# A third landing slot for weights, paid for with a staging slot, in a two-layer hybrid backbone

## The chip, the cores and the metric

The kernel runs on one core of one Trainium2 chip, as one launch. The metric is the device time of that launch in microseconds (us), less is better. The engines are named as in the profile: PE (TensorE, matrix products), PEld (its weight loads), DVE (VectorE), ACT (ScalarE), POOL (GpSimd) and SP (SyncE, which here only issues DMAs; SPq and ACTq are the queues of the two engines that issue them).

## The reference, cut to what matters

Two layers, each over 1024 latent tokens and 256 context tokens of width 1024, all in float32:

```python
for l in range(DEPTH):                                   # DEPTH = 2
    shift, scale, gate = split(silu(c) @ w_ada[l] + b_ada[l], 3)
    h = layer_norm(x) * (1 + scale) + shift              # the context rows likewise
    q, k, v, g_att, u_conv, g_conv, x_lru, g_lru = split_in_proj(h @ w_in[l])
    ys = window_attention(q, k, v, ...), conformer_conv(u_conv, ...), rglru(x_lru, ...)
    y = stack([yb * silu(gb) for yb, gb in zip(ys, gs)])   # three branches, 512 wide each
    proj = einsum('btnw,nwd->btnd', y, w_branch[l])
    g = sigmoid(h @ w_gate[l] + b_gate[l])                 # one gate per branch and channel
    out = sum(proj * g, branches) @ w_out[l]
    x = layer_norm(ALPHA * x + gate * out) * ln_g[l] + ln_b[l]
```

The big products are h with w_in (3840 columns) and w_gate (3072 columns), the branches with w_branch, and the merge with w_out.

## The kernel before

**Weights.** Every big product is made in three matmuls of a cheaper format: a float32 operand is split into a high part and the rest. A weight unit (class `Wt`, 128 x 1024 elements, 512 KB) goes through four steps in `Wt.load`: a DMA on SP into a tile `raw` (L332 is that DMA's line in the profile), a copy on ACT that rounds it to `whi`, a subtraction on DVE that leaves the rest in `wlo`, and then matmuls with both. Each of the three has a ring of slots in the pool W: `NWL` = 2 slots for raw, `NW` = 4 each for whi and wlo. A raw slot is free once the subtraction has read it; a whi and wlo slot is free once PE has used the unit. There are 180 such units. Four of each layer (half of w_out) live in another pool, RC, that is opened late in phase 2, and had `NW` = 4 raw slots there.

**Phase 1** of a layer (`phase1`) runs nine streams: gates, attention projection, scores, values and output, convolution, recurrence in, recurrence, recurrence out. `Driver.run` picks among them by its own cost estimates and emits their instructions in one long order. The products with w_gate and w_in interleave with all the rest. In layer 0 the gates' stream also computes the conditioning of layer 1 (`ada_pair`): two weight units of w_ada for each pair of column groups, used up in 32 short matmuls.

**Phase 2** (`phase2`) merges. The three branch outputs, which phase 1 left in DRAM (`yd`), come back in pieces of 128 x 512 through a ring of `NYST` = 3 staging slots (`yst`, L1156 is the DMA): `yfetch` fills the ring, `ysplit` splits one piece into high part and rest (ACT, then DVE; the tile is `yy`) and fetches the next. The order of branches is recurrence (i = 0), convolution (i = 1), attention (i = 2). The sigmoid values come back as `thl`. The sums of a row block stand in `m`: in tiles `mx` for latent tokens, and in a ring `mc` of four 2 KB slots for the context. Then come the two halves of the product with w_out, the second layer norm, and the transposed and modulated input of the next layer (`norm`: tiles `xp`, `hf`, `hlhi`). The tiles `tt` of the w_out product and `hf` share one ring of two slots in RC.

**Gate rows.** `gate_out` transposes the conditioning's gate into a row tile `grow`, copies it from PSUM on DVE and stores it to DRAM; `gate_in` later reads it back, spread over partitions. It is called at the start of the second and third quarter of branch i = 0. **First rows.** `load_c` brings the two conditioning vectors in at the very start, in tiles `crow` and `crow2`. All these row tiles are 512 bytes for each partition in a pool SM that stays open all the time.

**Order and waits.** Nothing in the code waits by hand. Tiles of one tag share that tag's slots, and an instruction that would write into a slot waits for the last reader of what stood there. The program is compiled with

```python
with _tile.TileContext(nc, schedule_with_timeline_sim=True) as tc:
```

so the order on each engine is not the order of emission: a list scheduler places each instruction when its operands and its slot are there in a simulated run, the earlier emitted first. What results is one fixed order for each engine and queue, and on the chip each of them works strictly through it: the profile shows an instruction that waits and everything behind it on its engine standing still. The pools s, h, a, b and c of the phases follow one another in the same memory, and a tile of a later pool waits for the tiles that lay there before.

Of the kernel before, what the change touches and what calls it, by code (L numbers as in the profile page):

```python
# [8 lines left out]
F32 = mybir.dt.float32  # L9
# [23 lines left out]
NT_1 = (2, C + 512, 512)  # L33

SLOT = 1408
NS, NHF, NW, NWL, NMX, NYST = 10, 14, 4, 2, 8, 3
LH = 6


# [150 lines left out]
def kernel(  # L190
# [14 lines left out]
    SM = ctx.enter_context(tc.tile_pool(name="small", bufs=1))  # L205
# [3 lines left out]
    def pad(pool_, n, tag):  # L209

        if n:
            pool.memset(pool_.tile([128, n // 4], F32, tag=tag, name=tag), 0.0)
# [6 lines left out]
    def f32(ap):  # L219
        return ap.bitcast(F32)  # L220

    def psum(n=512, name="ps"):
        return PM.tile([128, n], F32, tag="mm", name=name, bufs=4)
# [97 lines left out]
    class Wt:  # L321
# [6 lines left out]
            self.ap, self.ready = drv_.side(lambda: self.load(src, a, b, home or W))  # L328

        def load(self, src, a, b, home):  # L330
            raw = home.tile([128, a, b], F32, tag="raw", name="raw", bufs=NWL if self.own else NW)
            sp.dma_start(out=raw, in_=src)  # L332
            hi = home.tile([128, a, b], F32R, tag="whi", name="whi", bufs=NW)
            lo = home.tile([128, a, b], F32R, tag="wlo", name="wlo", bufs=NW)
            act.activation(out=hi, in_=raw, func=AF.Copy)
            dve.tensor_tensor(out=lo, in0=raw, in1=f32(hi), op=ALU.subtract)
            return hi, lo
# [14 lines left out]
    def split(src, hi, lo):  # L352
        act.activation(out=hi, in_=src, func=AF.Copy)
        dve.tensor_tensor(out=lo, in0=src, in1=f32(hi), op=ALU.subtract)
# [3 lines left out]
    sel = K.tile([4, 2], F32, tag="sel", name="sel")  # L358
    dve.tensor_tensor(out=sel, in0=ident[0:4, 0:2], in1=ident[0:4, 2:4], op=ALU.add)

    def load_c():
        rows = SM.tile([128, 128], F32, tag="crow", name="crow")
        sp.dma_start(out=rows[0:8], in_=c[0].rearrange("(r p) -> r p", p=128))
        sp.dma_start(out=rows[8:16], in_=c_ctx.rearrange("(r p) -> r p", p=128))
        t = SM.tile([128, 128], F32, tag="crow2", name="crow2")
        act.activation(out=t[0:16], in_=rows[0:16], func=AF.Tanh, scale=0.5)
        dve.scalar_tensor_tensor(out=t[0:16], in0=t[0:16], scalar=1.0, in1=rows[0:16], op0=ALU.add, op1=ALU.mult)
        dve.tensor_scalar(out=t[0:16], in0=t[0:16], scalar1=0.5, scalar2=None, op0=ALU.mult)
        ps = psum()
        pe.transpose(ps[:, 0:16], t[0:16], ident[0:16, 0:16])  # L370
        dve.tensor_copy(cs.rearrange("p k s -> p s k"), ps[:, 0:16].rearrange("p (s k) -> p s k", s=2))
        split(cs, csr[:, :, 0:2], csr[:, :, 2:4])
# [3 lines left out]
    def ada_fin(l, jjs, ps, rows, r):  # L376

        n = len(jjs) * 128
        act.activation(out=r[0:rows, 0:n], in_=ps[0:rows, 0:n], func=AF.Copy)
        for i in range(len(jjs)):  # L380
            pe.matmul(out=ps[:, 2 * i:2 * i + 2], lhsT=r[0:rows, i * 128:i * 128 + 128], rhs=sel[0:rows], start=True,
                      stop=True)
        part, m = jjs[0] // 8, len(jjs)
        dst = ada[l][:, jjs[0]:jjs[0] + m, :]
        bias = prm[l][:, P_ADA + jjs[0]:P_ADA + jjs[0] + m].unsqueeze(2).to_broadcast([128, m, 2])
        dve.scalar_tensor_tensor(out=dst, in0=ps[:, 0:2 * m].rearrange("p (m s) -> p m s", s=2),
                                 scalar=1.0 if part == 1 else 0.0, in1=bias, op0=ALU.add, op1=ALU.add)
        if part == 2:
            dve.tensor_scalar(out=dst, in0=dst, scalar1=0.25, scalar2=None, op0=ALU.mult)
# [35 lines left out]
    def alloc_h(ti, n):  # L425
        tg, b = ("hc", 2) if n == 256 else ("hl", 4)
        return tuple(H.tile([128, KD, n], F32R, tag=tg, name=f"{tg}{v}", bufs=b) for v in ("hi", "lo"))

    def emit_h0(R, P):
        tiles = [(ctxt, 0), (ctxt, 128)] + [(x, 128 * i) for i in range(8)]  # L430
        raws, xt = {}, {}
        nts = (NT_C, NT_0, NT_1)

        def load_x(i):
            t = R.tile([128, 2, 512], F32, tag="raw0", name="x0", bufs=17).rearrange("p a b -> p (a b)")
            sp.dma_start(out=t, in_=tiles[i][0][0, tiles[i][1]:tiles[i][1] + 128, :])
            xt[i] = t

        def load_ada(g, q):
            raws[g, q] = R.tile([128, 2, 512], F32, tag="raw0", name="raw0", bufs=17)  # L440
            sp.dma_start(out=raws[g, q], in_=w_ada[0][q * 256:q * 256 + 256, g * 512:g * 512 + 512].rearrange(
                "(k p) n -> p k n", p=128))

        rows_ = {}

        def ada_rows(g, q):
            if q == 0:
                rows_[g] = P.tile([128, 512], F32, tag="p0", name="pa", bufs=4)
            for k in range(2):
                pe.matmul(out=rows_[g][0:2], lhsT=cs[:, q * 2 + k, :], rhs=raws[g, q][:, k, :],  # L450
                          start=(q == 0 and k == 0), stop=(q == 3 and k == 1))
            if q == 3:
                ada_fin(0, [g * 4 + i for i in range(4)], rows_[g], 2,
                        R.tile([128, 512], F32, tag="hf0", name="arow", bufs=5))

        def norm_x(i):
            t = xt[i]
            mv, rs = ln_stats(t)
            nb = SM.tile([128, 1], F32, tag="nb", name="nb", bufs=3)
            dve.scalar_tensor_tensor(out=nb, in0=mv[:, 0:1], scalar=-1.0, in1=rs, op0=ALU.mult, op1=ALU.mult)  # L460
            act.activation(out=t, in_=t, func=AF.Identity, scale=rs, bias=nb)

        def modulate(j, nt):
            ti, t0, n = nt
            s = 1 if ti == 0 else 0
            ps = P.tile([128, 512], F32, tag="p0", name="p0", bufs=4)
            for i in range(n // 128):
                pe.transpose(ps[:, i * 128:i * 128 + 128], xt[t0 // 128 + i][:, j * 128:j * 128 + 128], ident)
            hf = R.tile([128, 512], F32, tag="hf0", name="hf0", bufs=5)
            act.activation(out=hf[:, 0:n], in_=ps[:, 0:n], func=AF.Identity, scale=ada[0][:, 8 + j, s:s + 1],  # L470
                           bias=ada[0][:, j, s:s + 1])
            hi, lo = (v[:, j, :] for v in hT[0, ti])
            if j < (4, 4, 6)[ti]:
                act.activation(out=hi, in_=hf[:, 0:n], func=AF.Copy)
            else:
                dve.tensor_copy(hi, hf[:, 0:n])
            dve.tensor_tensor(out=lo, in0=hf[:, 0:n], in1=f32(hi), op=ALU.subtract)

        load_c()
        for nt in nts:  # L480
            hT[0, nt[0]] = alloc_h(nt[0], nt[2])
            if nt is NT_C:
                pad(H, 64, "padh2")

        def rows_tile():
            return R.tile([128, 128], F32, tag="rows", name="rows", bufs=2)

        order = [("a", 0, 0), ("a", 0, 1), ("a", 0, 2), ("r",), ("a", 2, 0), ("a", 0, 3), ("a", 2, 1), ("a", 2, 2),
                 ("a", 2, 3), ("x", 0), ("x", 1), ("a", 1, 0), ("a", 1, 1), ("a", 1, 2), ("a", 1, 3), ("a", 3, 0),
                 ("a", 3, 1), ("a", 3, 2), ("a", 3, 3), ("m", NT_C, 0), ("m", NT_C, 4), ("x", 2), ("x", 3),  # L490
                 ("x", 4), ("x", 5), ("x", 8), ("m", NT_0, 0), ("m", NT_0, 4), ("x", 6), ("x", 9), ("x", 7),
                 ("m", NT_1, 0), ("m", NT_1, 4)]
        for what, *v in order:
            if what == "m":
                for j in range(v[1], v[1] + 4):
                    modulate(j, v[0])
            elif what == "r":
                load_params(0, *load_rows(0, rows_tile))
            elif what == "a":
                load_ada(*v)  # L500
                ada_rows(*v)
            else:
                load_x(*v)
                norm_x(*v)
# [622 lines left out]
        drv_.run([lru(), att_values(), att_scores(), lru_in(), lru_out(), att_proj(), att_out(), conv(), gates()], PRIO[l])  # L1127
        assert wlive[0] == 0 and sl.used == 0 and hl_.used == 0 and pl_.used == 0

    def gate_out(l, s):  # L1130

        row = SM.tile([128, 128], F32, tag="grow", name="grow")
        ps = psum()
        pe.transpose(ps[0:KD, 0:128], ada[l][:, 16:24, s], ident)
        dve.tensor_copy(row[0:KD], ps[0:KD, 0:128])
        sp.dma_start(out=gate_d[l][s].rearrange("(k p) -> k p", p=128), in_=row[0:KD])
# [5 lines left out]
    def phase2(l, open_a, open_b, open_c):  # L1142
# [24 lines left out]
        def mc(name):  # L1167
            return RB.tile([128, 512], F32, tag="mc", name=name, bufs=4)
# [52 lines left out]
        def gemm():  # L1221
# [3 lines left out]
            for i, b in enumerate(BR):  # L1225
                for dp in range(4):
                    if i == 0 and 0 < dp < len(groups):
                        gate_out(l, dp - 1)
                    if i == 0:
                        for nt in groups:  # L1230
                            if nt is NT_C:
# [232 lines left out]
```

## Time and profile before

| | |
|---|---|
| median of 3 runs | 2307.63 us (2306.44 to 2307.89) |
| time of the profiled execution | 2307.8 us |
| its span, first to last instruction | 2306.0 us |
| PE busy | 2249.3 us (98%) |
| DVE busy | 1678.9 us (73%) |
| ACT busy | 1003.4 us (44%) |
| mean granted TensorE clock | 0.990 |

The span is what the trace covers; 1.8 us of the profiled execution's time lie outside it. All times in the trace count from the first instruction. Almost every instruction has the line L73, which is the helper `Meter` that records costs; so the rows are read by the tiles, out<-in. Phase 1 of layer 0 begins at about 55 us, phase 2 is under way alone from 1021 us, layer 1 begins at about 1303 us, and its phase 2 at about 2078 us. Matmuls overlap in the pipeline, so PE's busy time counts small delays as work; idle times of PE are real.

### The profile page before, as it was taken

The page shows a single profiled execution, that of the slowest core. Times are in us where ns is not written, and L with a number is a line of the kernel's source. Part 1 is how long each engine was busy: PE and PEld are TensorE (multiplying, and loading weights), DVE is VectorE, ACT ScalarE, POOL GpSimd, SP SyncE. Part 2 cuts the span into 40 slices and gives each one's busy share as a digit, 9 for nine tenths or more (in the row PEclk, how much of TensorE's full clock was granted, in tenths as well). Part 3 has the DMA queues.
Part 4 walks back from the last instruction along what each step waited for, and adds up shares of the span by engine and source line. Part 5 has one row for each costly group of instructions (what it writes and reads, how often), then busy time and mean ns, then how long its engine had stood idle before and what let it go on. Part 6 is the DMA issues. An engine that isn't in the chain of part 4 may idle for free.

```text
span 2306.0 us, 29961 instructions
## 1 busy us (share of the span) xinstructions
PE 2249.3 (98%) x11344; PEld 1871.8 (81%) x11344; DVE 1678.9 (73%) x2453; ACT 1003.4 (44%) x1642; POOL 86.7 (4%) x140
## 2 busy tenths in 40 slices
PE   7999999999999999999999999999999999999998
PEld 2888888888888887888888788888888878778886
DVE  5579967868959875545678749869778787655667
ACT  4555563245444575422122644565344456542110
POOL 1000000000000111000001100000000011000002
PEclk8999999999999999999999999999999999999999
DMA  7223323433334232655562222233423334347532
GB/s 276 76 73 101 115 73 126 142 112 108 108 101 138 80 117 87 203 167 168 151 206 74 94 66 67 80 92 128 142 90 97 89 122 131 111 136 227 160 128 92
DMA packets 270946, 279.90 MB, mean 121 GB/s; under 512 B 19769, under 2 KB 199889, under 8 KB 270801
## 3 DMA queue, kind: packets, MB, share of 16 engines
q1 hardware_dynamic: 242288, 226.06, 31.4%
q10 hardware_dynamic: 28512, 51.92, 6.4%
q8 instruction: 89, 1.46, 0.3%
q14 instruction: 57, 0.46, 0.1%
HBM read 203.04 MB, written 74.88 MB: 121 GB/s over the span
## 4 chain that ended last, share of the span: by engine, by line
PE 88%; DVE 5%; ACT 2%; DMA 2%; issue 2%; SPq 0%; POOLq 0%; POOL 0%; ACTq 0%; DVEq 0%
PE ps L73 82%; PE yp L73 3%; PE pt L73 2%; PE pa L73 1%; DVE acc L73 1%; DMA raw<-in_w_ada_dram 1%; DVE P L73 1%; DVE pl L73 1%; DVE wlo L73 1%; DMA yst<-yd 1%; ACT whi L73 0%; DMA qd<-qd 0%; DVE xp L73 0%; PE p L73 0%; ACT hf L73 0%
## 5 line engine op out<-in xcount | busy, mean ns | idle before, releaser
L73 PE MATMUL ps<-hlhi,whi 128*128 128x512 f32 x1728 | 681.9, 395 | 2.2 <-DVE gs L73 1.0
L73 PE MATMUL ps<-hllo,whi 128*128 128x512 f32 x1728 | 678.4, 393 | 0.0
L73 PE MATMUL ps<-hlhi,wlo 128*128 128x512 f32 x1728 | 676.8, 392 | 0.0
L73 PEld LDWEIGHTS ps<-hlhi,wlo 128*128 128x128 f32 x1728 | 325.8, 189 | 67.5 <-issue 0.4
L73 PEld LDWEIGHTS ps<-hlhi,whi 128*128 128x128 f32 x1728 | 326.5, 189 | 66.5 <-DVE pl L73 2.2
L73 PEld LDWEIGHTS ps<-hllo,whi 128*128 128x128 f32 x1728 | 326.2, 189 | 62.7 <-issue 0.7
L73 DVE SCALAR_TENSOR_TENSOR acc<-u,cwt,acc 128x1296 f32<-128x1296 f32 (+1 forms) x240 | 342.3, 1426 | 2.2
L73 ACT ACTIVATE whi<-raw 128x1024 fp32r<-128x1024 f32 x180 | 190.0, 1058 | 334.1 <-PE ps L73 299.9
L73 DVE TENSOR_TENSOR wlo<-raw,whi 128x1024 fp32r<-128x1024 f32 x180 | 220.4, 1225 | 95.1 <-ACT whi L73 91.5
L73 PE MATMUL ps<-yy,whi 128*128 128x512 f32 (+1 forms) x960 | 271.6, 368 | 2.8 <-DVE m L73 2.8
L73 PEld LDWEIGHTS ps<-yy,whi 128*128 128x128 f32 x960 | 173.7, 188 | 33.5 <-DVE m L73 3.2
L73 PE MATMUL ps<-yy,wlo 128*128 128x512 f32 (+1 forms) x480 | 176.6, 368 | 0.0
L73 ACT ACTIVATE ph<-pt 128x512 fp32r<-128x512 f32 x160 | 93.9, 591 | 130.5 <-PE pt L73 125.1
L73 DVE TENSOR_TENSOR pl<-pt,ph 128x512 fp32r<-128x512 f32 x160 | 108.9, 685 | 50.8 <-ACT ph L73 49.4
L73 PE MATMUL ps<-hchi,whi 128*128 128x256 f32 x480 | 135.6, 283 | 1.3 <-ACT whi L73 0.5
L73 ACT ACTIVATE P<-P,nm 128x640 f32<-128x640 f32 (+1 forms) x128 | 101.9, 798 | 79.7 <-DVE nm L73 79.6
L73 PE MATMUL ps<-hchi,wlo 128*128 128x256 f32 x480 | 135.3, 282 | 1.0 <-DVE wlo L73 1.0
L73 PE MATMUL ps<-hclo,whi 128*128 128x256 f32 x480 | 134.6, 281 | 0.0
L73 DVE CUSTOM_DVE_ANT_0 P<-ps,m_mid,nsink 128x640 f32<-128x640 f32 (+1 forms) x112 | 93.0, 859 | 42.3 <-PE ps L73 40.8
L73 ACT ACTIVATE tg<-ps,drv 128x512 f32<-128x512 f32 (+1 forms) x120 | 76.4, 637 | 68.3 <-PE ps L73 67.7
L73 PEld LDWEIGHTS ps<-yy,wlo 128*128 128x128 f32 x480 | 90.5, 188 | 15.0
L73 PE MATMUL pt<-ident,P 128*128 128x128 f32 x640 | 97.2, 274 | 3.1 <-DVE pl L73 1.4
(205 smaller groups left out, 3396.1 us busy)
## 6 DMA issues: line engine op xcount, KB each, us to landing
raw<-in_w_in_dram SPq DMA_DIRECT2D x60, 512.0 KB
raw<-in_w_ada_dram SPq DMA_DIRECT2D x48, 512.0 KB
raw<-in_w_gate_dram SPq DMA_DIRECT2D x48, 512.0 KB
th<-tg ACTq DMA_DIRECT2D x96, 256.0 KB
thl<-th SPq DMA_DIRECT2D x96, 256.0 KB
yd<-gs ACTq DMA_DIRECT2D x48, 256.0 KB
yst<-yd SPq DMA_DIRECT2D x48, 256.0 KB
raw<-in_w_branch_dram SPq DMA_DIRECT2D x24, 512.0 KB
```

Of the source, the lines that this page charges most:

```text
L73: return f(*a, **k)
```

## The change

Four edits. In the pool W the ring raw gets three slots instead of two, and in the pool RC it gets three instead of four (`bufs=NWL` for both). The staging ring yst goes from three slots to two. The tiles crow and crow2 move from SM to R, the pool of the first stage, which is closed after it. The tile grow moves from SM to the ring mc, which keeps its four slots. Each raw slot takes 4 KB in a partition, each yst slot 2 KB; the permanent pools grow by 2.5 KB.

```diff
-NS, NHF, NW, NWL, NMX, NYST = 10, 14, 4, 2, 8, 3
+NS, NHF, NW, NWL, NMX, NYST = 10, 14, 4, 3, 8, 2
...
         def load(self, src, a, b, home):
-            raw = home.tile([128, a, b], F32, tag="raw", name="raw", bufs=NWL if self.own else NW)
+            raw = home.tile([128, a, b], F32, tag="raw", name="raw", bufs=NWL)
...
-    def load_c():
-        rows = SM.tile([128, 128], F32, tag="crow", name="crow")
+    def load_c(R):
+        rows = R.tile([128, 128], F32, tag="crow", name="crow")
...
-        t = SM.tile([128, 128], F32, tag="crow2", name="crow2")
+        t = R.tile([128, 128], F32, tag="crow2", name="crow2")
...
-        load_c()
+        load_c(R)
...
-    def gate_out(l, s):
-
-        row = SM.tile([128, 128], F32, tag="grow", name="grow")
+    def gate_out(l, s, row):
+
...
-                        gate_out(l, dp - 1)
+                        gate_out(l, dp - 1, mc("grow")[:, 0:128])
```

## Rows read from the trace of the kernel before

**Rows 1.** The page, part 1: busy us, share of the span, instructions.

```profile
PE 2249.3 (98%) x11344; PEld 1871.8 (81%) x11344; DVE 1678.9 (73%) x2453; ACT 1003.4 (44%) x1642; POOL 86.7 (4%) x140
```

**Rows 2.** Waits of PE: who waited for whom, total us, times, longest.

```profile
PE yp L73 <- ACT ph L73: 9.1, 9, 2.3
...
PE ps L73 <- DVE wlo L73: 1.0, 2, 0.8
...
PE ps L73 <- ACT whi L73: 0.5, 2, 0.3
```

**Rows 3.** Waits of all engines, same columns.

```profile
ACT whi L73 <- PE ps L73: 299.9, 83, 12.9
...
ACT whi L73 <- DMA raw<-in_w_ada_dram: 8.7, 5, 2.8
...
ACT whi L73 <- DMA raw<-in_w_in_dram: 7.6, 5, 2.7
```

**Rows 4.** ACT in order of time, conditioning stretch: start, us, what, [idle before].

```profile
567.36 1.06 ACT L73 ACTIVATE whi<-raw 128x1024 fp32r<-128x1024 f32 x1 [2.20 <-DMA raw<-in_w_ada_dram]
...
569.13 0.57 ACT L73 ACTIVATE ph<-pt 128x512 fp32r<-128x512 f32 x1
...
591.38 1.06 ACT L73 ACTIVATE whi<-raw 128x1024 fp32r<-128x1024 f32 x1 [2.78 <-DMA raw<-in_w_ada_dram]
...
593.15 0.58 ACT L73 ACTIVATE ph<-pt 128x512 fp32r<-128x512 f32 x1
```

**Rows 5.** PE in order of time, same stretch.

```profile
567.73 0.60 PE L73 MATMUL pt<-ident,P 128*128 128x128 f32 x4
...
569.76 0.50 PE L73 MATMUL yp<-ph,vs 128*128 128x512 f32 x1 [1.20 <-ACT ph L73]
...
590.66 0.60 PE L73 MATMUL pt<-ident,P 128*128 128x128 f32 x4
...
593.78 0.79 PE L73 MATMUL yp<-ph,vs 128*128 128x512 f32 x1 [2.29 <-ACT ph L73]
```

**Rows 6.** The chain that ended last: start, us, what.

```profile
585.38 5.97 DMA raw<-in_w_ada_dram
...
1027.02 3.35 DMA yst<-yd
...
1303.97 0.68 DVE xp L73
```

**Rows 7.** Windows: stretch, us, busy PE, PEld, DVE, ACT, POOL, PEclk, DMA, GB/s.

```profile
560.00:600.00 40.00, 36.51 (x213) 30.74 (x211) 38.26 (x51) 19.26 (x37) 0.00 (x0) 0.96 0.40 122
593.50:597.00 3.50, 3.22 (x8) 2.54 (x9) 3.43 (x6) 1.20 (x4) 0.00 (x0) 0.51 0.51 148
600.00:750.00 150.00, 149.97 (x877) 128.15 (x876) 118.12 (x182) 69.23 (x137) 0.20 (x3) 1.00 0.38 116
```

**Rows 8.** ACT in order of time where layer 1 begins.

```profile
1303.67 1.06 ACT L73 ACTIVATE whi<-raw 128x1024 fp32r<-128x1024 f32 x1 [2.74 <-DMA raw<-in_w_in_dram]
1304.64 2.88 ACT L73 ACTIVATE hf<-ps,ada 128x128 f32<-128x128 f32 x8
```

**Rows 9.** PE in order of time, same place.

```profile
1301.99 1.91 PE L73 MATMUL ps<-ident,xp 128*128 128x128 f32 x16
...
1312.53 1.97 PE L73 MATMUL ps<-ident,xp 128*128 128x128 f32 x8 [3.86 <-ACT hf L73]
```

**Rows 10.** PE in order of time, where branch pieces are staged.

```profile
1032.13 0.73 PE L73 MATMUL ps<-yy,whi 128*128 128x512 f32 x2 [2.46 <-DVE m L73]
```

**Rows 11.** Waits of SP's queue, columns as in rows 2.

```profile
SPq L332 <- DVE wlo L73: 812.1, 139, 26.3
...
SPq L1156 <- DVE yy L73: 25.8, 35, 1.7
SPq L1156 <- DMA yd<-gs: 25.1, 5, 8.2
```

**Rows 12.** The tile grow: duration ns min/median/max, first and last start.

```profile
L73 DVE COPY grow<-ps x3: 272/272/274, 1038.5 to 2094.4; 8x128 f32<-8x128 f32 x3
```

## The prediction, made before the changed kernel ran

> **What bounds the kernel now.** I read the page's first part, then the waits of PE, then those of the other engines, then the timelines of the places where PE stands still. PE is busy for 2249.3 of 2306.0 us [rows 1]; so a change that moves no matmul can only win from the 56.7 us of idle time, from stretches at the low clock, and from small delays that the overlap hides. Of that idle time PE's direct waits for a weight unit are a sliver: 0.5 us for the rounded part and 1.0 us for the rest; its largest waiter is the attention product, 9.1 us in nine waits for `ph`, the rounded probabilities that ACT makes [rows 2]. ACT's waits for weights tell why the units are seldom late: 299.9 us in 83 waits before a `whi` end with PE, which means that the raw unit had landed and the slot of whi was what was missing; 8.7 and 7.6 us, ten waits, end with a load in phase 1 or at its border [rows 3]. The third raw slot can act only on those ten, on PE's 1.5 us, and on what stands behind them in ACT's queue.
>
> **The third raw slot, where PE feels it.** Two of the ten waits lie in the conditioning of layer 1, where a pair of w_ada units follows a gate unit and is used up at once. At 565.16 and at 588.60 ACT comes to a split whose load is not there, and stands still for 2.20 and 2.78 us; behind the split in its queue wait an exponential and `ph` [rows 4]. The four transposes that ph reads are done at 568.33 and at 591.26, and PE then waits 1.20 and 2.29 us for ph [rows 5]. The second load began at 585.38, the moment its slot was given back, and took 5.97 us [rows 6]. With a slot more a load begins one release earlier. At the pace of 877 matmuls in 150 us [rows 7] a gate unit with its 72 matmuls is 12 us of PE, so I take the wait as gone. What is late next is the transposes themselves: ph can start at 568.33 instead of 569.13, and at 591.26 instead of 593.15. So PE wins 0.80 + 1.89 = 2.69 us, not the full 3.49. The second stop is followed by a stretch of 3.5 us in which the granted clock is 0.51 of full speed, the lower of its two levels, and at 1.00 later [rows 7]; with PE idle for 0.4 us instead of 2.3 before it I expect the fall to stay out, which gives back 3.5 x 0.49 = 1.7 us. Together 4.4 us. Bounds: nothing, if another engine holds the same PE (below), and 3.49 + 1.7 = 5.2.
>
> PE's direct waits, 1.5 us, I take as gone too: bounds 0 and 1.5. From 600 to 750 us ACT has more waits of this kind, but PE is busy there for 149.97 of 150.00 us [rows 7]: worth nothing in PE's idle time, whatever ACT wins.
>
> **Where layer 1 begins.** The fourth split there waits 2.74 us for its load and ends when `hf` begins, at 1304.64 [rows 8]. This looks like a gain: the first eight of the transposes that hf reads were over by about 1303 us (sixteen take 1.91 us from 1301.99), and later PE waits 3.86 us for hf [rows 9]. But hf takes its memory from the two-slot ring of `tt`, and the chain goes through DVE's last reading of a tt, 1303.97 to 1304.65, into hf [rows 6]. So hf starts no earlier, and I count nothing. Bounds: a gain of 1304.64 - 1303 = 1.6 us if another tt slot was free; a loss of about a split, 1.06 us, if the fourth unit's subtraction now stands ahead of that reading on DVE, which has no pause there.
>
> **The raw ring in RC** goes from four slots to three. The fourth of these loads must now wait until the first unit is split: one split (1.06 us) and its subtraction, then a load of up to 5.97 us [rows 4, 6], some 9 us. It is hidden by the first half of the product, 4 row blocks of 24 matmuls in layer 0 and 6 in layer 1: at the pace above 96 take 16 us. Without that cover it would cost up to 9 us, in each layer.
>
> **Two staging slots.** A piece's slot is held for its load (3.35 us for the one on the chain [rows 6]) and the split. At 1029.67 PE runs out of PSUM: DVE's merge `m` stands behind the split of the piece whose load began at 1027.02, and PE waits 2.46 us [rows 10]. With two slots such a piece comes later or its neighbours do. Bound above: 12 pieces for each branch in layer 0, by loads alone 12 x 3.35 / 3 = 13.4 us with three slots and 20.1 with two, 6.7 us if all of it showed; in layer 1 eight pieces, 8.9 and 13.4, 4.5 us. Below: nothing, since in five cases a load waits for the branch's own store (25.1 us), not for a slot, and the slot waits of this queue add up to 25.8 us in 35 short pieces of at most 1.7 [rows 11]. The next branch's pieces are split while PE works through a whole branch, so only a merge that gets stuck behind a split costs anything. I take half as much again as the stop of today, since each slot turns 3 / 2 as often: 2.46 x 0.5 = +1.2 us.
>
> **The row tiles.** Three copies to grow, 0.27 us each [rows 12], and their three stores are the same as before, on the same queues. In `mc` the row takes a slot that a context sum needs one quarter of a branch later; it is free when the store has landed, and the quarter's 72 matmuls (12 us by the pace above) cover a small store: nothing, and at most one load's 3 us without the cover. crow and crow2 lie in a pool that is open and empty when they are loaded: nothing.
>
> **Sum.** -4.4 - 1.5 + 0 + 1.2 = -4.7 us on the span of 2306.0: 2301.3. With the 1.8 us outside the span 2303.1; the profiled execution (2307.8) is 0.2 above the median of the runs, so 2302.9 us.
>
> **The rivals.**
> *No change, because DVE takes over.* DVE is busy for 38.26 of the 40 us around both stops [rows 7]. Attention's product needs DVE's half of the probabilities as well, and if that comes when ACT's half came before, the 4.4 us are lost: 2307.6 - 1.5 + 1.2 = 2307.3. For it: DVE's load. Against: the waits end with ACT, and DVE's fillers are convolution taps that can go later. The same result follows if the next thing missing is a whi slot and not the load, as in 83 waits against ten [rows 3].
>
> *Much faster.* If every wait of ACT for a load stood for PE time somewhere, 16.3 us [rows 3], the time would be 2307.6 - 16.3 + 1.2 = 2292.5. This asks also that SP's queue becomes free. SP stands before a raw load, waiting for the subtraction that gives its slot back, for 812.1 us [rows 11], and loads of attention wait behind it. Against: the third slot changes which unit a freed slot serves, not that SP waits for each release in turn, so what is behind it waits as before. The Trainium skill (DMA: Bandwidth & Descriptors, Anatomy of one DMA) has it that a DMA's semaphore wait takes place on the issuing sequencer before dispatch; by that rule alone a deeper ring frees nothing behind SP's waits, and the trace agrees with its 812.1 us. Hence its small chance.
>
> *Slower by the order.* The order of each engine is planned; a unit that lands earlier in the plan is split earlier in ACT's and DVE's fixed order. Each split that so gets in front of an evacuation that PE waits for costs 1.06 us on ACT [rows 4]. The place is the conditioning stretch, 32 units of w_ada. To end above 2312.2 it must eat the 4.7 and 4.6 more: nine such splits; with twelve, 2302.9 + 12.7 = 2315.6.
>
> *Slower by staging.* All of 6.7 + 4.5 us shows: 2307.6 - 5.9 + 11.2 = 2312.9. For it: the one stop that exists. Against: pieces are split ahead of need.
>
> **How the numbers follow.** 0.2%, about what a measurement of this kernel can tell from no change, is 4.6 us: faster is below 2303.0, slower above 2312.2. The forecast has 0.41, its own range 2298 to 2306, and lies at the border, mostly under it, since other short delays in the overlap go the same way: 0.33 faster, 0.08 the same. No change has 0.26. Much faster 0.13. Slower by the order 0.12, by staging 0.08. So faster 0.46, same 0.34, slower 0.20. The range goes from the fullest gain, 2291, to staging fully exposed, 2313; beyond it I leave the worst order and a larger gain than any wait shows.
>
> **What the profile after would show.** Right: no wait of ACT's whi for w_ada near 567 and 591 us, PE's waits for ph there under 0.5 us, and no stretch at half clock behind; the waits of whi for loads down from 16.3 us to a few; SP's waits at the raw loads still near 800 us; PE idle from 1010 to 1035, where 2.46 us are one stop now, between 2.5 and 5 us. Wrong: PE waiting for `pl` of DVE at those two places; idle time of PE in phase 2 grown by more than 5 us; ACT's splits standing ahead of evacuations, with PE's waits for ACT grown elsewhere. What would make the whole prediction wrong is a new order that opens or closes stops of 2 us and more, each with a stretch at half clock behind it, in places that no edit touches.

## The result: slower by 12.6 us, and the profile after

The changed kernel takes 2320.41 us (median of 4 runs, 2318.91 to 2320.88) against 2307.76 us of the kernel before on the same chip (2306.44 to 2308.19): a ratio of 1.0055, 95% interval 1.004 to 1.007. The prediction had 2302.9 us and a range up to 2313.

The page of the changed kernel, part 1, answers to [rows 1]:

```profile
span 2318.5 us, 29983 instructions
...
PE 2258.7 (97%) x11344; PEld 1878.3 (81%) x11344; DVE 1678.0 (72%) x2453; ACT 1004.4 (43%) x1642; POOL 87.0 (4%) x140
```

The span grew by 12.5 us. PE is busy 9.4 us longer with the same 11344 matmuls, and its idle time went from 56.7 to 2318.5 - 2258.7 = 59.8 us, only 3.1 more. Most of the longer busy time with equal work is the clock. In the first execution of each kernel, the stretches in which the granted clock is at the lower of its two levels (apart from the one behind the last matmul) add up to 41.0 us in six before and to 58.0 us in eleven after; 17.0 us more at half speed are 8.5 of the 9.4, if PE is taken as busy all through them. Counting only the time in which PE is busy inside them, 30.1 us before and 48.1 after, it is 9.0.

Where does it arise? The same matmuls, found in both traces, give the difference so far. The last `arow` transposes of the conditioning (one tile's instructions, first and last start), before and after:

```profile
L73 PE MATMUL ps<-sel,arow x64: 246/246/268, 104.8 to 735.8; 4*128 4x2 f32 x64
```

```profile
L73 PE MATMUL ps<-sel,arow x64: 246/246/267, 105.2 to 741.4; 4*128 4x2 f32 x64
```

and PE in order of time, three known waits of phase 2 and of the end of layer 1's phase 1; first two rows of before (the third is [rows 10]), then the changed kernel:

```profile
2053.53 0.50 PE L73 MATMUL yp<-ph,vs 128*128 128x512 f32 x1 [1.48 <-ACT ph L73]
...
2089.90 0.73 PE L73 MATMUL ps<-yy,whi 128*128 128x512 f32 x2 [0.30 <-DVE m L73]
```

```profile
1040.58 1.19 PE L73 MATMUL ps<-yy,whi 128*128 128x512 f32 x2 [2.28 <-DVE m L73]
...
2063.39 0.49 PE L73 MATMUL yp<-ph,vs 128*128 128x512 f32 x1 [1.48 <-ACT ph L73]
...
2101.75 0.28 PE L73 MATMUL ps<-ident,ada 128*8 128x128 f32 x1 [0.80 <-DVE m L73]
2102.35 0.73 PE L73 MATMUL ps<-yy,whi 128*128 128x512 f32 x2 [0.32 <-DVE m L73]
```

The changed kernel is 0.4 us late at the first `arow`, 5.6 at the last, 8.45 at the staging stop (1040.58 against 1032.13), 9.86 at the wait for ph, 12.45 at the staging place of layer 1. So two thirds arise in layer 0's phase 1, and almost nothing (1.4 us) between 1032 and 2053 us.

**The place where 4.4 us were to be won.** Waits of PE, and then of all engines, columns as in [rows 2]; they answer to [rows 2, 3]:

```profile
PE pt L73 <- DVE pl L73: 5.8, 3, 3.6
PE yp L73 <- ACT ph L73: 4.4, 5, 1.5
...
PE ps L73 <- DVE yt L73: 2.2, 1, 2.2
```

```profile
ACT whi L73 <- DMA raw<-in_w_in_dram: 2.6, 2, 1.5
```

ACT's waits for w_ada loads are gone, those for w_in fell from 7.6 to 2.6 us, and PE's for ph from 9.1 to 4.4. In their place stands `pl`, DVE's half of the probabilities: 5.8 us in three waits, where before there was one of 1.4. PE, ACT and DVE in order of time, the stretch of [rows 4, 5]:

```profile
567.24 0.50 PE L73 MATMUL yp<-ph,vs 128*128 128x512 f32 x1
571.34 1.12 PE L73 MATMUL pt<-ident,P 128*128 128x128 f32 x4 [3.59 <-DVE pl L73]
...
594.90 0.40 PE L73 MATMUL yp<-ph,vs 128*128 128x512 f32 x1
596.48 0.76 PE L73 MATMUL pt<-ident,P 128*128 128x128 f32 x4 [1.19 <-DVE pl L73]
```

```profile
562.45 2.01 ACT L73 ACTIVATE whi<-raw 128x1024 fp32r<-128x1024 f32 x2 [0.46 <-PE ps L73]
...
565.50 0.58 ACT L73 ACTIVATE ph<-pt 128x512 fp32r<-128x512 f32 x1
```

```profile
566.03 0.89 DVE L73 CUSTOM_DVE_ANT_0 P<-ps,m_mid,nsink 128x640 f32<-128x640 f32 x1
...
566.84 2.37 DVE L73 TENSOR_TENSOR wlo<-raw,whi 128x1024 fp32r<-128x1024 f32 x2
569.11 1.57 DVE L73 SCALAR_TENSOR_TENSOR acc<-u,cwt,acc 128x1296 f32<-128x1296 f32 x1
570.59 0.70 DVE L73 TENSOR_TENSOR pl<-pt,ph 128x512 fp32r<-128x512 f32 x1
```

Read them backwards. The transposes at 571.34 need the PSUM tile that `pl` reads last. pl could have begun at 566.08, when ph was done; it begins at 570.59, because the fixed order of DVE puts a step of the scores (P, 0.89 us), two subtractions (2.37) and a convolution tap (1.57) first. The two subtractions stand together because the two splits do (`x2` at 562.45 on ACT), and these because both w_ada units of the pair have landed (SP issues their two loads together at 542.88, where the kernel before issues them at 545.44 and 562.57): the change at work. In the kernel before, DVE subtracts the two units of this pair one at a time, each time with pl right behind it:

```profile
565.54 1.22 DVE L73 TENSOR_TENSOR wlo<-raw,whi 128x1024 fp32r<-128x1024 f32 x1
566.68 0.69 DVE L73 TENSOR_TENSOR pl<-pt,ph 128x512 fp32r<-128x512 f32 x1
...
568.90 1.22 DVE L73 TENSOR_TENSOR wlo<-raw,whi 128x1024 fp32r<-128x1024 f32 x1
570.03 0.69 DVE L73 TENSOR_TENSOR pl<-pt,ph 128x512 fp32r<-128x512 f32 x1
```

Windows (columns as in [rows 7]) over the same stretch, the fall of the clock inside the stop, and the one behind the second stop:

```profile
560.00:600.00 40.00, 35.22 (x197) 29.77 (x195) 38.46 (x52) 20.64 (x39) 0.00 (x0) 0.88 0.40 121
569.60:576.40 6.80, 5.06 (x14) 4.20 (x15) 6.65 (x11) 2.51 (x5) 0.00 (x0) 0.50 0.51 163
596.90:600.30 3.40, 3.40 (x11) 2.73 (x10) 3.40 (x6) 2.01 (x4) 0.00 (x0) 0.50 0.87 278
```

The first stop is 3.59 - 1.20 = 2.4 us longer, and 5.06 us of matmuls behind it run at the lower level, which costs 2.5 more: 4.9 us. The second is 1.1 us shorter, and has its half-clock stretch all the same. Matched matmuls agree: the changed kernel is 0.2 us early at 550 us and 3.5 late at 600.

**Two stops later.** DVE in order of time near 743 and 817 us, the kernel before:

```profile
734.92 1.22 DVE L73 TENSOR_TENSOR wlo<-raw,whi 128x1024 fp32r<-128x1024 f32 x1
736.06 0.68 DVE L73 TENSOR_TENSOR pl<-pt,ph 128x512 fp32r<-128x512 f32 x1
...
809.47 1.48 DVE L73 TENSOR_SCALAR P<-P,es 128x640 f32<-128x640 f32 x3
810.87 0.85 DVE L73 TENSOR_TENSOR yt<-yp,yt 64x256 f32<-64x256 f32 x2
...
812.95 1.23 DVE L73 TENSOR_TENSOR wlo<-raw,whi 128x1024 fp32r<-128x1024 f32 x1 [0.26 <-ACT whi L73]
```

and the changed kernel:

```profile
742.13 1.22 DVE L73 TENSOR_TENSOR wlo<-raw,whi 128x1024 fp32r<-128x1024 f32 x1
743.27 0.68 DVE L73 TENSOR_TENSOR pl<-pt,ph 128x512 fp32r<-128x512 f32 x1
...
816.16 1.22 DVE L73 TENSOR_TENSOR wlo<-raw,whi 128x1024 fp32r<-128x1024 f32 x1
817.30 0.85 DVE L73 TENSOR_TENSOR yt<-yp,yt 64x256 f32<-64x256 f32 x2
```

and PE behind them, before (no wait at the first place) and after:

```profile
737.06 0.60 PE L73 MATMUL pt<-ident,P 128*128 128x128 f32 x4
```

```profile
744.01 0.66 PE L73 MATMUL pt<-ident,P 128*128 128x128 f32 x4 [1.00 <-DVE pl L73]
...
818.30 0.35 PE L73 MATMUL ps<-hchi,whi 128*128 128x256 f32 x1 [2.18 <-DVE yt L73]
```

Near 817 a subtraction has moved ahead: before, `yt` follows a step of the probabilities at once and the subtraction comes behind it; now the subtraction stands between them, and PE waits 2.18 us for yt. Behind this stop the clock is at 0.50 from 818.8 to 822.2. Near 743 the order of DVE is the same in both kernels. There DVE is 7.2 us later than before (742.13 against 734.92) and PE, at its last `arow`, only 5.6, so PE waits 1.00 us for a pl that used to be done in time. The order did change further ahead (two subtractions stand together at 715.34 and 716.48, before at 711.16 and 714.69 with pl between them); that this is what put DVE behind is not shown.

Matched matmuls give what the places are worth in these two executions: 3.7 us from 550 to 600 us, 1.5 at 744, 2.8 at 817 with the stretch behind it, 0.7 near 915, about 2 in small steps between 600 and 740, and a gain of 1.8 near 795, where the half-clock stretch is 3.4 us long and was 6.8.

### The profile page after: what moved, and what is told of

Same layout as the page of the kernel before. It is cut to its first block, busy times and chain, and to the rows that moved or that the text cites. A ratio compares the mean times of both kernels' runs of the same rounds, so it can differ in the third digit from the quotient of the medians.

```text
span 2318.5 us, 29983 instructions
## 1 busy us (share of the span) xinstructions
PE 2258.7 (97%) x11344; PEld 1878.3 (81%) x11344; DVE 1678.0 (72%) x2453; ACT 1004.4 (43%) x1642; POOL 87.0 (4%) x140
## 4 chain that ended last, share of the span: by engine, by line
PE 87%; DVE 6%; DMA 3%; ACT 2%; issue 2%; SPq 0%; POOL 0%; POOLq 0%; ACTq 0%; DVEq 0%
PE ps L73 80%; PE yp L73 3%; PE pt L73 2%; DVE acc L73 1%; PE pa L73 1%; DMA yst<-yd 1%; DVE wlo L73 1%; DVE P L73 1%; DVE pl L73 1%; DMA raw<-in_w_ada_dram 0%; ACT whi L73 0%; DVE yt L73 0%; DVE xp L73 0%; DMA raw<-in_w_in_dram 0%; DMA qd<-qd 0%
```

## The experiments

Theories: **A**, the third slot lets units land together, and their subtractions stand ahead of pl and yt on DVE. **B**, any edit that reshuffles the planned order costs this much, wherever it is. **C**, the two staging slots are the loss. **D**, part of the difference is half-clock stretches that a stop of the same length has behind it in one execution and not in another. Runs e1 to e13 were made on four chips (e1 to e4, e5 to e8, e9 to e11, e12 and e13); there the kernel before has medians of 2309.4 to 2311.9 us, against 2307.76 beside the first result, and each ratio is against the kernel before on the same chip. The diffs are shortened to the lines that matter, with `...` in some of them; marks like `# e3` say which run a line belongs to.

**e1: the rows and the ring of RC alone.** The changed kernel with

```diff
-NS, NHF, NW, NWL, NMX, NYST = 10, 14, 4, 3, 8, 2
+NS, NHF, NW, NWL, NMX, NYST = 10, 14, 4, 2, 8, 3
-            raw = home.tile(..., bufs=NWL)
+            raw = home.tile(..., bufs=NWL if self.own else 3)
```

> The kernel before with the row tiles crow, crow2 and grow moved and the ring of RC at three slots; W's raw ring stays at two, yst at three. Theory A (the loss comes from the third raw slot in W: both w_ada splits come together, DVE's two subtractions stand ahead of its half of the probabilities, the stop is longer and half-clock stretches follow): no change, 2307.8 us within 3. Theory B (the loss is a general reshuffle of the planned order that any of the edits can set off): a loss or gain of 5 us or more here too. Theory C (the staging ring is the loss): no change.

Measured 2310.55 us, 0.9998 (0.9988 to 1.0008): nothing, as A and C have it. PE's order is that of the kernel before, but for three matmuls near 1300 us.

**e2: two staging slots alone.** As e1, with NYST = 2 and four slots in RC.

> The row tiles moved and the staging ring at two slots; W's raw ring at two, RC's at four. Theory A: the idle time of PE grows only where the second layer's phase 2 stages its pieces, 1 us near 2097 us, so 2308 to 2310 us. Theory C: at least half of the 12.6 us, 2314 us or more. Theory B: 5 us either way, in places that have nothing to do with staging.

Measured 2313.46 us, 1.0006 (0.9997 to 1.0015): 1.4 us by the ratio, which the interval does not tell from nothing. C falls. The order of SP's and DVE's instructions did change here, though only from 941 us on, and costs at most 0.15% by the interval: B in its bare form falls too. On what a change of order in layer 0's phase 1 costs, this run says nothing, for there was none.

**e3, e4: the w_ada subtractions made differently.** e3 keeps them in the order of emission, e4 gives them to POOL:

```diff
-            dve.tensor_tensor(out=lo, in0=raw, in1=f32(hi), op=ALU.subtract)
+            i = dve.tensor_tensor(out=lo, in0=raw, in1=f32(hi), op=ALU.subtract)     # e3
+            if self.ada: tc.keep_in_program_order(i)
+            (pool if self.ada else dve).tensor_tensor(out=lo, ...)                   # e4
```

> The changed kernel, with the subtractions of the w_ada units kept in the order of emission on DVE. Theory A: the stop of 3.59 us near 571 us, where PE waits for pl of DVE, and the 6.8 us at half clock behind it go; layer 0's phase 1 gives back most of its 8.6 us, 2311 to 2314 us in all, with the 1.4 and 1.6 us at 1034 and 2057 us left. Theory B: another order, so another set of stops: anything from 2308 to 2325 us, and stops where no w_ada unit is. Theory C: no change, 2320 us.

> The changed kernel, with the subtractions of the w_ada units on POOL, which is busy for 87 us of the whole span, in place of DVE. Theory A: pl follows P at once on DVE, PE waits under 0.5 us for it near 567 and 591 us, no half-clock stretch there: 2308 to 2314 us, unless POOL takes so much longer for a subtraction than DVE's 1.19 us that PE waits for wlo. Theory B: 2308 to 2325 us with stops elsewhere. Theory C: 2320 us.

Measured 2353.14 us, 1.0181 (1.0166 to 1.0196), and 2362.10 us, 1.0227 (1.0211 to 1.0243). Both miss what every theory gave. In e3 the subtractions now come late, three in a row, and PE stands still for the first (DVE and PE in order of time):

```profile
738.79 3.49 DVE L73 TENSOR_TENSOR wlo<-raw,whi 128x1024 fp32r<-128x1024 f32 x3
```

```profile
740.07 0.37 PE L73 MATMUL ps<-wlo,csr 128*4 128x256 f32 x1 [4.27 <-DVE wlo L73]
```

In e4 POOL needs 2.85 us for what DVE does in 1.22 (groups by line), PE waits 10.9 us in five waits for `arow`, which comes out of these units, and the plan is another one throughout:

```profile
L337 POOL TENSOR_TENSOR wlo<-raw,whi 128x1024 fp32r<-128x1024 f32 x32 | 90.9, 2846 | 569.2 <-ACT whi L73 389.5 <-PE ps L73 59.0 <-PE pt L73 39.9
```

They tell nothing against A, for they moved the lateness instead of taking it away; e3 shows that here a change of when some subtractions run is worth 42 us against the kernel before; in e4 (51 us) they also take more than twice as long.

**e5 to e7: the changed kernel again, and the third slot for one kind of unit.** e6 was to skip the third slot for the second w_ada unit by taking an unused tile; e7 gives the third slot to that unit alone:

```diff
-            raw = home.tile([128, a, b], F32, tag="raw", name="raw", bufs=NWL)
+            raw = home.tile(..., tag="rawx", bufs=1) if self.x else home.tile(..., tag="raw", bufs=NWL - 1 if self.own else NWL)
```

> The changed kernel once more, beside the other runs of this call on one chip. All theories: 1.004 to 1.007 of the kernel before.

> The changed kernel, in which an unused raw tile is taken before the second w_ada unit of each pair: that unit then has to wait for the subtraction two units earlier, as with two slots; the other units keep three. Theory A (the pair landing together is the cause): layer 0's phase 1 loses its 8.6 us; no stop of 3.59 us near 571; 2308 to 2313 us on the chip of the first measurement, 0.3 to 0.55% less than the changed kernel. Theory B (any reshuffle of the order): another set of stops; no tie to the pair; anywhere from 1.000 to 1.010. If the third slot for the other units is the cause: as the changed kernel, 1.0055.

> The changed kernel with the third raw slot kept for the second w_ada unit of each pair alone (a ring of its own with one slot); the others take turns in two. Theory A: as the changed kernel, 1.004 to 1.007, with the long stop near 571 us and half clock behind it. If the third slot for the other units is the cause: 1.000 to 1.002. Theory B: anywhere.

Measured: e5 2319.80 us, 1.0038 (1.0024 to 1.0051), just under the 1.004 that was expected; e6 2321.10 us, 1.0042 (1.0029 to 1.0054); e7 2318.81 us, 1.0037 (1.0025 to 1.0050). In e6 the unused tile took no slot: PE's and DVE's order is the changed kernel's, so it is no more than a third execution of that. e7, too, is just under A's 1.004, and level with e5: the third slot at the second unit of a pair is enough for a loss of this size. The changed kernel itself takes as long here as in the first result (2320.41 us); what is longer is the kernel before, 2311.33 us in place of 2307.76. So of the first 12.6 us some 4 depend on which runs of the kernel before stand beside it.

**e8: the kernel before, once more in profile.** No edit.

> The kernel before, profiled once more on this chip. Theory D (part of the difference is half-clock stretches that a stop of the same length has behind it or not, by its place in time): the same stops of 2.46 us near 1030 us and 1.65 and 1.73 us near 2045 and 2051 us, and half-clock stretches that are not all the ones of the first execution; where the stretches are the same, the time is the same within 0.5 us. If the stretches are a fixed consequence of the stops: the same list.

One run, 2309.11 us, span 2307.3. The stretches at half clock are the same six as in the first execution, each about 0.9 us later, as a fixed consequence of the stops would have it, so this run says nothing for D; the staging stop is 2.21 us, and the stops of this program differ between the two executions as well (PE's wait for ph near 570 us is 0.57 us here and was 1.20). The changed kernel does say it (below).

**e9, e10: two slots while a pair is fetched; three slots in layer 1 alone.** In e9 a raw slot is held by a tile that POOL writes and reads (one element) until the subtraction two units earlier is done; in e10 every third unit of layer 1 takes the extra slot:

```diff
+            if self.x:                                                                # e9
+                hold = home.tile([128, a, b], F32, tag="raw", name="hold", bufs=NWL)
+                pool.memset(hold[0:1, 0, 0:1], 0.0)
+                pool.tensor_tensor(out=hold[0:1, 0, 0:1], in0=hold[0:1, 0, 0:1], in1=f32(los[-2])[0:1, 0, 0:1], op=ALU.add)
+            x = self.own and lay[0] and len(cnt) % 3 == 2; cnt.append(0)              # e10
+            raw = home.tile(..., tag="rawx" if x else "raw", bufs=1 if x else NWL - 1 if self.own else NWL)
```

> The changed kernel; before the second w_ada unit of each pair is loaded, one raw slot is taken by a tile that POOL writes (one element) and reads again only after the subtraction two units earlier: while a pair is fetched there are two slots, else three. Theory A (the pair landing together puts subtractions ahead of pl and yt on DVE): the stop of 3.6 us near 571 us and the half-clock stretch behind it go, 1.000 to 1.002 of the kernel before. Theory B (any reshuffle of the planned order costs, whatever is reshuffled): stops of 2 us and more elsewhere, 1.003 to 1.010. If the third slot for the other units costs by itself: 1.003 or more, with the stops where w_in and w_gate units are split.

> The changed kernel, with two raw slots in layer 0 and three from layer 1 on (every third unit of layer 1 takes the extra one). Theory A: layer 0 as in the kernel before, layer 1 without effect but for the staging, 1.000 to 1.0015. Theory B: a loss of 3 us or more in layer 1 too, where the order changes as well.

Measured: e9 2316.61 us, 1.0026 (1.0014 to 1.0038); e10 2314.90 us, 1.0019 (1.0011 to 1.0028). In e9 the stop of 3.6 us is gone, as A has it, and the ratio is lower than e5's by 0.0012, though the intervals overlap; the two later stops stay, which A had not foreseen, and the ratio is above A's 1.002. In e10 none of the three is there, and layer 1 has no new stop but at its staging; the ratio is a little above A's 1.0015. But layer 0 did not stay as it was: the extra slot is free from the start, and in e10 a third load goes out at 40.49 us, before any subtraction has given a slot back (the first one begins at 48.68). From there on the order differs from the kernel before, and PE waits 1.33 us for pl at 630 us, where the kernel before has no wait. So 4.4 us by the ratio, half of e5's loss, are there without any of the three stops; e2's staging may be 1.4 of them, and the rest is open.

**e11: the w_ada subtractions in two halves.**

```diff
+                for r in range(0, a, 2):
+                    dve.tensor_tensor(out=lo[:, r:r + 2], in0=raw[:, r:r + 2], in1=f32(hi[:, r:r + 2]), op=ALU.subtract)
```

> The changed kernel, with each subtraction of a w_ada unit made in two halves of 128 x 512. Theory A, if what hurts is the length of the block ahead of pl: pl can slip in between, the waits of PE for pl and yt in layer 0's phase 1 fall by a third or more, 1.002 to 1.004. Theory B: as large a loss as the changed kernel or larger, 1.004 to 1.02, with the waits in other places and not tied to the pair.

Measured 2331.45 us, 1.0082 (1.0066 to 1.0097), twice the loss. PE's waits are spread anew: `pl` 9.0 us up to 1000 us, and 2.8, 3.3 and 2.1 us for ACT's `tg`, `rstd` and `ph` between 835 and 1000 us, where the changed kernel has 0.5 us for ph and none for the others. A's 1.002 to 1.004 is missed, and this is B's case: an edit of the subtraction's cost makes another plan.

**e12, e13: the third slot only early, only late.** Every third unit takes the extra slot, in e12 among the first 66 units (loaded before about 640 us), in e13 from there on:

```diff
+            x = self.own and len(cnt) < 66 and len(cnt) % 3 == 2; cnt.append(0)       # e12; e13: >= 66
+            raw = home.tile(..., tag="rawx" if x else "raw", bufs=1 if x else NWL - 1 if self.own else NWL)
```

> The changed kernel with the third raw slot for the first 66 weight units alone (those loaded before about 640 us), two after. If each stop comes from the ring's depth where it stands: the stop of 3.6 us near 571 us stays, those near 743 us (pl behind a subtraction) and 816 us (yt behind a subtraction) go; 1.001 to 1.003. If an early shift of the planned order carries them (one reshuffle, many places): all three stay, and 1.0035 to 1.006, as the changed kernel.

> The changed kernel with two raw slots for the first 66 weight units and three from there on. If each stop comes from the ring's depth where it stands: no stop of 3.6 us near 571 us, those near 743 and 816 us there; 1.001 to 1.004. If an early shift of the planned order carries them: none of the three, 1.000 to 1.0015.

Measured: e12 2320.03 us, 1.0036 (1.0024 to 1.0049); e13 2318.69 us, 1.0031 (1.0019 to 1.0043). By its stops e12 lies between the two theories, and its ratio is in the range of the second; e13 is as the first has it. PE in order of time at the three places, e13 and then e12:

```profile
572.36 0.50 PE L73 MATMUL yp<-ph,vs 128*128 128x512 f32 x1 [1.85 <-ACT ph L73]
...
744.27 0.66 PE L73 MATMUL pt<-ident,P 128*128 128x128 f32 x4 [1.00 <-DVE pl L73]
...
816.98 0.36 PE L73 MATMUL ps<-hchi,whi 128*128 128x256 f32 x1 [2.18 <-DVE yt L73]
```

```profile
573.11 1.11 PE L73 MATMUL pt<-ident,P 128*128 128x128 f32 x4 [3.50 <-DVE pl L73]
...
819.28 0.36 PE L73 MATMUL ps<-hchi,whi 128*128 128x256 f32 x1 [2.15 <-DVE yt L73]
```

All runs at the three places (waits of PE in us; "ph" is the old wait for ACT):

| third raw slot | near 571 | near 744 | near 817 | ratio |
|---|---|---|---|---|
| nowhere (before; in e8 ph 0.57) | ph 1.20 | none | none | 1 |
| everywhere (the change, here e5; first execution pl 3.59) | pl 3.23 | pl 1.00 | yt 2.18 | 1.0038 |
| second w_ada unit only (e7) | pl 3.38 | none | yt 2.16 | 1.0037 |
| first 66 units (e12) | pl 3.50 | none | yt 2.15 | 1.0036 |
| all but that w_ada unit (e9) | ph 1.54 | pl 1.01 | yt 2.18 | 1.0026 |
| from unit 67 on (e13) | ph 1.85 | pl 1.00 | yt 2.18 | 1.0031 |
| layer 1 only (e10) | ph 2.01 | none | none | 1.0019 |

The stop near 571 goes with the slot's use by the pair, the one near 744 with its use by other units from 640 us on: each comes from the ring's depth at its own place, as A, widened to all units, has it. The one near 817 comes with either, which neither theory explains; it stays open. The stops do not add up to the ratios, whose intervals overlap in most rows: the table shows where each stop comes from, not what share of the loss it has. In e13, as in e10, the first load into the extra slot goes out at 40 us, and PE waits 1.22 us at 631 us, ahead of the units that were to have it. e9, e12 and e13 show that no part of the third slot in layer 0 is a gain, and no version here beats the kernel before.

**D, from executions of one program.** The changed kernel (first execution) and e5 have the same instructions in the same order, and the same waits of 2.28 or 2.03 us at the staging stop and twice 1.48 us near 2060. Windows just behind those two places, first the changed kernel, then e5:

```profile
1040.70:1044.00 3.30, 3.30 (x8) 2.62 (x9) 1.76 (x4) 1.04 (x2) 0.00 (x0) 0.50 0.87 282
2064.70:2068.00 3.30, 3.30 (x11) 2.65 (x10) 1.61 (x3) 0.91 (x2) 0.10 (x1) 0.50 0.79 242
```

```profile
1040.00:1043.30 3.30, 3.30 (x15) 2.73 (x16) 2.21 (x5) 1.26 (x2) 0.00 (x0) 1.00 0.80 261
2062.80:2066.10 3.30, 3.30 (x18) 2.72 (x18) 1.66 (x3) 0.96 (x2) 0.10 (x1) 1.00 0.79 227
```

Half clock behind both places in the one, full clock in the other: in 3.30 us PE starts 8 and 11 matmuls, or 15 and 18. Over the whole program the stretches add up to 58.0, 51.2 and 61.4 us in three executions of the changed kernel (first, e5, e6), with spans of 2318.5, 2315.2 and 2319.2; the first two differ by 6.8 us of half clock, worth 3.4, and by 3.3 us of span. The twelve runs of e9, again one program, go from 2310.97 to 2322.01 us: the six shortest have a mean granted clock of 0.989 to 0.991, the six longest 0.987 or 0.988. The Trainium skill (TensorE: Matmul & The Clock Gate, Part 1) says of the slow matmuls with which a kernel starts that their number varies from run to run, since what the gate looks at is not tied to the kernel's start; these executions show such a spread behind later stops.

## Why the prediction was wrong

**The step that failed** is in the third raw slot: "What is late next is the transposes themselves", priced at -2.69 us of stops and -1.7 us of half clock. That the wait for the load would go was right: ACT's waits for w_ada went from 8.7 us to none, PE's for ph at the two places from 1.20 and 2.29 to none. But what is late next is `pl`. The step looked at ACT's queue alone; the subtraction of a unit that lands earlier moves up on DVE too, and DVE has work for 38 of the 40 us. So instead of -4.4 the two places bring 2.4 + 2.5 - 1.1 = +3.8 us, worked out from the rows above. That this stop goes with the slot is shown by e9 and e13 (without) and e7 and e12 (with); that it is the larger part of the loss is not, for e10 has half of the loss without it.

**The rivals.** "Slower by the order" named the mechanism (splits ahead of evacuations in a fixed order) and the side, at 0.12; it put it on ACT, at 1.06 us a split and nine of them, where it is DVE's subtraction, at two places (waits of 3.59 and 2.18 us) and perhaps indirectly at a third (1.00), and the clock makes it dearer. It too came out too low: 2315.6 with twelve splits. "No change, because DVE takes over" had the engine and the tile, pl, but let it only cancel the gain. The sign that was named for it ("PE waiting for `pl` of DVE at those two places") is what the profile shows.

**The clock** was counted for one stop only. Of the 12.5 us, 8.5 to 9.0 are matmuls at half clock. Part follows from the longer stops (569.6, 818.8 us); part, about 3 us in the first execution (the 1.4 between 1032 and 2053 us, and 1.7 of the 2.6 between 2053 and 2090: 3.4 us at half clock from 2064.6), stands behind stops that the change did not lengthen, and is absent in e5. That is the case which the prediction ended with, a new order with stops of 2 us and a stretch at half clock behind, and to which it gave no chance of its own.

**Direct waits of PE for weights**, -1.5: the two waits for wlo, 1.0 us, are gone, of 0.5 for whi 0.3 stay. A new wait of 2.2 us for whi at 54 us stands where the kernel before waits 1.7 for hf. So the step won its 1.0, and the start gave half of it back.

**Layer 1's start**, 0: right. The two waits for hf, 0.94 and 3.86 us (the second is in [rows 9]), became 0.99 for hf, 2.46 for hlhi and 0.49 for hllo, 3.94 in place of 4.80; but the same matmuls are 10.0 us late ahead of this place and 9.9 behind it.

**Staging**, +1.2: about right in size, by luck, for it lies in another place. At the stop of [rows 10], which the step made half as long again, nothing was added (2.28 after 2.46); in layer 1, 0.80 + 0.32 stand against 0.30 us. e2 alone has +1.4 us by its ratio, not told from nothing by its interval.

**RC, rows**, 0: right, by e1. ACT's waits for the loads of w_out grew from 7.0 to 11.3 us, and PE did not feel it: the same matmuls are 10.0 us late from 1050 to 1300 us. **SP** stands 788.3 us before raw loads, 812.1 before: a deeper ring freed next to nothing there, as argued.

## What to carry over

Where the order on each engine is planned and fixed, a buffer that lets an operand land earlier moves up every instruction that reads it, on each engine that does; look in the trace for what stands behind those instructions on the busiest engine, here DVE at 38 of 40 us, and not only at the engine that waited. Price a stop with the half-clock stretch that may follow (in the changed kernel behind stops of 1.0 to 3.6 us), and expect such stretches to come and go between executions of one program. An edit of one operation's cost or place in such a plan is no clean experiment (e3, e4, e11). Changing the ring's depth for chosen units comes nearer, but look whether the plan changed elsewhere too: in e10 and e13 the extra slot moved a load to 40 us and with it the order of layer 0.

## What the runs showed of the hardware, unexpected

The clock fell behind stops of 2.28 and 1.48 us in one execution and stayed at 1.00 behind the same stops, 2.03 and 1.48 us, in another. And POOL slows DVE: with the subtractions on POOL (e4) the taps of layer 0 take 1714 ns in the mean, 1562 before (groups by line and shape, e4 and then before), the longest of them 3.70 us in place of 1.57; layer 1's taps, with no subtraction beside them, are unchanged at 1291 ns. Of the 120 taps of layer 0 the 20 that overlap a subtraction on POOL take 2476 ns in the mean, the other 100 1561.

```profile
L73 DVE SCALAR_TENSOR_TENSOR acc<-u,cwt,acc 128x1296 f32<-128x1296 f32 x120 | 205.6, 1714 | 1.0
```

```profile
L73 DVE SCALAR_TENSOR_TENSOR acc<-u,cwt,acc 128x1296 f32<-128x1296 f32 x120 | 187.4, 1562 | 0.8
```

The Trainium skill (SBUF — State Buffer, SBUF: two separate sides) has the two engines share a pair of ports that a DVE instruction with two SBUF inputs and a GpSimd instruction that reads SBUF take in turns, each for its whole length; a tap reads two tiles, and the trace agrees in direction, 18.2 us over 120 taps.
